# Second sample group's value tiles: four buffers of the key pool in place of the shared work pool

## The chip, the cores and the metric

One NeuronCore of one Trainium2 chip runs the whole program. The metric is device time in microseconds (us), from the start to the end of one execution; the figure that counts is the median of several executions. Beside it stands one execution that the hardware profiler recorded instruction by instruction; every row below is of that one.

## The reference

The program is one inference step of a decoder layer for a prompt (1 sequence of 512 tokens) and a sample group (8 sequences, b = 0..7, with 4 new tokens each), 1024 wide: a half-weighted SwiGLU block, then dilated attention (8 heads of 64) beside an S5 state-space group, a second half-weighted SwiGLU block, a gated projection and a final norm. The change concerns the attention of the sample group over its cache of 2048 old positions:

```
for window, dil in ((128, 1), (512, 4), (2048, 16)):
    idx = past + t - arange(window // dil + 1) * dil      # keys that new token t sees in this branch
    logits = q[t] . k_ext[idx] / 8 + bias ;  probs = softmax(logits)
    o = sum(probs * v_ext[idx])
merged = softmax-weighted sum of the three branches' o
```

So every sample sequence needs, of its cached values, the last 128 rows, and per new token 128 rows 4 apart and 128 rows 16 apart.

## The kernel before

All activations stay on chip. The program goes through a first feed-forward part, a mixing part (projections, prompt attention, sample attention, S5), and a second feed-forward part with the final output. In the mixing part the order of work on TensorE, VectorE, ScalarE and GpSimd is written out by hand: a string ORDER names, one after the other, steps of generators, and each engine works through its own list strictly in that order. `M` and `E` are weight matmul tiles and their evacuation, `aq`, `at`, `ap` are the three steps of a unit of prompt attention (scores with softmax, transposes, values), `SQ` multiplies cached keys by queries, `O0` and `O1` are the sample outputs of the sequences 0 to 3 and 4 to 7 (`sample_out(0)` and `sample_out(1)`, 15 steps each).

`sample_out(gr)` first makes the softmax weights of its four sequences (tiles `pz` and `sc`), then goes through nine value steps, n = 0 to 8: step 0 is the last 128 rows, steps 1 to 8 are (token, branch) pairs. Each step has two value tiles `vv` of 128 x 2 x 512 floats (512 KB), one for each pair of sequences, loaded by a DMA that GpSimd issues (line 1178). They are called 0a, 0b, 1a, 1b, ... 8a, 8b below. In step n the program first issues load n+1 (both tiles), and then TensorE multiplies the weights with both tiles of step n into one accumulator `po` (line 1191). Since a DMA is issued by GpSimd's own in-order list, a load whose buffer is not yet free holds up all that GpSimd has behind it; behind the loads of the second group stand only two `bt` loads (bias rows of prompt attention, line 1003, between 0b and 1a) and, much later, additions of the next norm.

Where a tile lies is decided by its pool. `wk` takes from a pool of six buffers (`wkp`, WK = 6) that also serves the S5 tiles earlier and `pz`; `kk2` takes from a pool of four buffers of the same size (`kkp`), used until then by the stream of cached keys in `SQ`, whose last multiplication stands before the second group's value steps. A new tile takes a buffer that its last tile has given back in program order, and its load waits until that tile's last reader is done. One of the six work buffers is held by the second group's `pz` until its last value step. The lines in question:

```python
        kkp = st.enter_context(tc.tile_pool(name="kkp", bufs=4))
        wk = lambda shape, name: wkp.tile(shape, F32, name=name, tag="wk")
        kk2 = lambda name: kkp.tile([P, 2, DA], F32, name=name, tag="kk")
```

Of the kernel before, what the change touches and what calls it, by code (L numbers as in the profile page):

```python
# [18 lines left out]
P = 128  # L19
# [9 lines left out]
DA = 512  # L29
# [73 lines left out]
def decoder_step(ctx: ExitStack, tc: tile.TileContext, a: dict, o: list):  # L103
# [3 lines left out]
    def dram(t, off, dims):  # L107
        return bass.AP(tensor=t.tensor, offset=t.offset + off, ap=dims)
# [6 lines left out]
    def sb(pool, shape, name, dt=F32, **kw):  # L115
        return pool.tile(shape, dt, name=name, **kw)
# [195 lines left out]
    def s2(shape, name, dt=F32):  # L312
        return cur["s2"].tile(shape, dt, name=name, tag="s2")

    def psm(shape=None, name="sm"):
        return cur["sm"].tile(shape or [P, 512], F32, name=name, tag="sm")
# [425 lines left out]
    with ExitStack() as st:  # L742
# [7 lines left out]
        wk = lambda shape, name: wkp.tile(shape, F32, name=name, tag="wk")  # L750
        s5 = lambda shape, name: sp5.tile(shape, F32, name=name, tag="s5")
        kk2 = lambda name: kkp.tile([P, 2, DA], F32, name=name, tag="kk")
# [380 lines left out]
        def sample_out(gr):  # L1133
            sc = scs[gr]
            s3 = lambda i, n=P: sc[:n, i].rearrange("p b (t h) -> p (b t) h", h=NH)
            bq = lambda t: t[:, None, :].to_broadcast([P, 16, NH])
            fs = lambda i, n=P: sc[:n, i].rearrange("p b x -> p (b x)")
            V.tensor_tensor(s3(0), s3(0), bq(bfar), ALU.add)
            V.tensor_tensor(s3(1), s3(1), bq(bnear), ALU.add)
            mx = s2([P, P], "mx")  # L1140
            V.tensor_tensor(mx, fs(1), fs(2), ALU.max)
            V.tensor_tensor(mx, mx, fs(0), ALU.max)
            V.tensor_tensor(mx[:NS], mx[:NS], fs(3, NS), ALU.max)
            yield
            ps = psm()
            PE.transpose(ps[:, :P], mx, ident)
            m1 = sb(small, [P, 4], "m1", bufs=2)
            V.tensor_reduce(m1[:, 0:1], ps[:, :P], AX.X, ALU.max)
            dg = sb(small, [P, P], "diag", bufs=2)
            V.tensor_scalar(dg, ident, m1[:, 0:1], None, ALU.mult)  # L1150
            yield
            pm = psm()
            PE.matmul(pm[:, :P], ones, dg, start=True, stop=True)
            for i, n_ in ((0, P), (1, P), (2, P), (3, NS)):
                V.tensor_tensor(fs(i, n_), fs(i, n_), pm[:n_, :P], ALU.subtract)
            pz = wk([P, 2, 4, 160], "pz")
            pz = [pz[:, i] for i in range(2)]
            dv = lambda t: t.rearrange("p b (t x) -> p b t x", x=40)[:, :, :, 0:8]
            s4v = lambda i, n=P: sc[:n, i].rearrange("p b (t h) -> p b t h", h=NH)
            for i in range(2):  # L1160
                V.memset(pz[i], 0.0)
                A.activation(dv(pz[i]), s4v(i), AF.Exp)
            A.activation(fs(2), fs(2), AF.Exp)
            A.activation(fs(3, NS), fs(3, NS), AF.Exp)
            yield
            su = s2([P, 4, 4, 8], "su")
            V.tensor_tensor(su, s4v(2), dv(pz[1]), ALU.add)
            V.tensor_tensor(su, su, dv(pz[0]), ALU.add)
            V.tensor_tensor(su[:NS], su[:NS], s4v(3, NS), ALU.add)
            order = [None] + [(j, f) for j in range(DS) for f in range(2)]  # L1170
            vld = {}

            def load(n):
                if n < len(order):
                    r0, step = (1920, 1) if n == 0 else ((order[n][0], 16), (1536 + order[n][0], 4))[order[n][1]]
                    vld[n] = [wk([P, 2, DA], "vv") for _ in range(2)]
                    for e in range(2):
                        Q.dma_start(vld[n][e], dram(cv, ((4 * gr + 2 * e) * PAST + r0) * DA,  # L1178
                                                    [[step * DA, P], [PAST * DA, 2], [1, DA]]))
            load(0)  # L1180
            yield
            ps = psm()
            PE.matmul(ps[:, 0:1], su.rearrange("p b t h -> p (b t h)"), ones[:, 0:1], start=True, stop=True)
            V.reciprocal(m1[:, 1:2], ps[:, 0:1])
            po = psm([P, 512], "po")
            for n, jf in enumerate(order):
                load(n + 1)
                v_ = vld.pop(n)
                for b in range(4):
                    lt = sc[:, 2, b] if n == 0 else pz[jf[1]][:, b, 32 * jf[0]:32 * jf[0] + 32]  # L1190
                    PE.matmul(po[32 * b:32 * b + 32, :], lt, v_[b // 2][:, b % 2, :], start=n == 0, stop=n == len(order) - 1)  # L1191
                if n == 0:
                    for b in range(4):
                        PE.matmul(po[32 * b:32 * b + 32, :], sc[:NS, 3, b], vs, start=False, stop=False)
                yield
            rv = s2([P, NH, HD], "rvv")
            V.scalar_tensor_tensor(rv, po.rearrange("p (h d) -> p h d", d=HD), m1[:, 1:2],
                                   sel_h[:, :, None].to_broadcast([P, NH, HD]), ALU.mult, ALU.mult)
            yield
            pf = psm([P, 4, 16], "pf")  # L1200
            for m in range(4):
                PE.matmul(pf[:, m, :], rv[:, 2 * m:2 * m + 2, :].rearrange("p h d -> p (h d)"), sel_t, start=True, stop=True)
            V.tensor_copy(att[:, :, S + 16 * gr:S + 16 * gr + 16], pf)
            yield
# [274 lines left out]
```

## Time and profile before

| | us |
|---|---|
| median of 3 runs | 1298.36 |
| lowest and highest | 1295.39, 1302.9 |
| the profiled execution's own time | 1290.02 |
| its span, first to last instruction | 1288.2 |
| TensorE busy in it | 1208.3 (94%) |
| mean granted TensorE clock | 0.968 |

The profiled execution is 8.3 us under the median and 5.4 us under the lowest of the three runs, so a sum of stalls read from it is compared with its own 1290.02 and then carried over to the median. Times in rows are us from the start of its span. The names PE, DVE, ACT, POOL and SP stand for TensorE, VectorE, ScalarE, GpSimd and SyncE; the second sample group's value steps lie between 719 and 764 us.

### The profile page before, as it was taken

To read this page: it belongs to the slowest core of one execution; us is meant where nothing else is said; L and a number is where in the kernel's file an instruction comes from. 1 tells how busy PE (TensorE), PEld (TensorE's weight loads), DVE (VectorE), ACT (ScalarE), POOL (GpSimd) and SP (SyncE) were. 2 spreads that over 40 slices of the span, in tenths; PEclk is the share of its full clock that TensorE was granted. 3 is DMA by queue.
4 is the path that set the end of the run, shared out by engine and by line. 5 is a ranking of instruction groups with operands and counts; after the bars stand their busy time and mean duration, and the time that the engine had idled before them with its cause. 6 is when DMAs were issued, how large, how long until landed. Compare 5 with 4: busy or idle time off the path is not lost.

```text
span 1288.2 us, 23223 instructions
## 1 busy us (share of the span) xinstructions
PE 1208.3 (94%) x9518; PEld 1142.4 (89%) x9518; DVE 713.5 (55%) x1499; ACT 446.1 (35%) x889; POOL 121.8 (9%) x195
## 2 busy tenths in 40 slices
PE   8999999999999999994769889999999999999995
PEld 7899999999999988983645449999999999999994
DVE  5544478476447638777775548444433444444455
ACT  5333322322233323121754445333322223333344
POOL 2200000233000112110123311000000000000000
PEclk8999999999999998996979989999999999999998
DMA  8484566668546549766358855445566455222321
GB/s 248 134 260 147 173 217 226 227 198 258 191 167 207 170 138 299 233 203 218 91 207 243 255 172 191 155 144 199 174 217 231 153 192 180 80 83 77 93 64 70
DMA packets 207547, 231.30 MB, mean 180 GB/s; under 512 B 8647, under 2 KB 187735, under 8 KB 206416
## 3 DMA queue, kind: packets, MB, share of 16 engines
q1 hardware_dynamic: 189552, 170.35, 40.8%
q0 software_dynamic: 17856, 59.45, 14.3%
q8 instruction: 75, 1.23, 0.4%
q14 instruction: 32, 0.26, 0.1%
q10 hardware_dynamic: 32, 0.01, 0.0%
HBM read 217.46 MB, written 81.89 MB: 232 GB/s over the span
## 4 chain that ended last, share of the span: by engine, by line
PE 81%; DMA 6%; DVE 5%; issue 4%; ACT 3%; POOL 1%; SPq 0%; ACTq 0%; POOLq 0%; DVEq 0%
PE acc L194 72%; DMA vv<-in_cache_v_dram 2%; DMA raw<-in_w_in_dram 1%; PE acc L206 1%; PE acc L1441 1%; DVE kk L1099 1%; DMA raw<-in_ffn_w_up_dram 1%; DMA pc<-pD 1%; PE sm L915 1%; PE po L1191 1%; DMA mm<-mD 1%; PE sm L910 1%; PE sm L263 1%; POOL vv L1178 1%; ACT L L1022 1%
## 5 line engine op out<-in xcount | busy, mean ns | idle before, releaser
L194 PE MATMUL acc<-xh,whi 128*128 128x272 f32 x1888 | 398.5, 292 | 5.9 <-DVE qT L773 1.3
L194 PE MATMUL acc<-xl,whi 128*128 128x272 f32 x1888 | 393.9, 290 | 0.7 <-DVE xl L304 0.3
L194 PE MATMUL acc<-xh,wlo 128*128 128x272 f32 x1888 | 393.4, 289 | 0.9 <-DVE wlo L176 0.9
L175 ACT CAST whi<-raw 128x512 fp32r<-128x512 f32 (+2 forms) x348 | 208.3, 606 | 531.1 <-PE acc L194 462.0
L176 DVE TENSOR_TENSOR wlo<-raw,whi 128x512 fp32r<-128x512 f32 (+2 forms) x348 | 231.1, 671 | 200.7 <-ACT whi L175 198.2
L194 PEld LDWEIGHTS acc<-xh,whi 128*128 128x128 f32 x1888 | 297.4, 189 | 12.0 <-issue 4.0
L194 PEld LDWEIGHTS acc<-xl,whi 128*128 128x128 f32 x1888 | 299.0, 190 | 1.9 <-DVE xl L304 0.8
L194 PEld LDWEIGHTS acc<-xh,wlo 128*128 128x128 f32 x1888 | 297.7, 189 | 1.4 <-DVE wlo L176 1.3
L194 PE MATMUL acc<-hh,whi 128*128 128x272 f32 x704 | 145.7, 288 | 0.0
L194 PE MATMUL acc<-hh,wlo 128*128 128x272 f32 x704 | 145.3, 288 | 0.0
L194 PE MATMUL acc<-hl,whi 128*128 128x272 f32 x704 | 145.2, 288 | 0.0
L194 PEld LDWEIGHTS acc<-hh,whi 128*128 128x128 f32 x704 | 110.7, 188 | 0.0
L194 PEld LDWEIGHTS acc<-hh,wlo 128*128 128x128 f32 x704 | 110.7, 188 | 0.0
L194 PEld LDWEIGHTS acc<-hl,whi 128*128 128x128 f32 x704 | 110.5, 188 | 0.0
L362 DVE TENSOR_TENSOR s<-acc,rstd 128x544 f32<-128x544 f32 x44 | 31.9, 724 | 87.3 <-PE acc L194 87.3
L356 DVE TENSOR_TENSOR s<-acc,rstd 128x544 f32<-128x544 f32 x44 | 31.9, 724 | 72.1 <-PE acc L194 65.9
L303 ACT CAST hh<-s 128x544 fp32r<-128x544 f32 x44 | 28.5, 647 | 78.9 <-DVE s L363 78.9
L304 DVE TENSOR_TENSOR hl<-s,hh 128x544 fp32r<-128x544 f32 x44 | 31.9, 725 | 27.3 <-ACT hh L303 27.3
L370 DVE SCALAR_TENSOR_TENSOR x<-acc,x 128x544 f32<-128x544 f32 x32 | 23.2, 725 | 36.0 <-PE acc L194 36.0
L1099 DVE TENSOR_TENSOR kk<-kk,qb 128x1024 f32<-128x1024 f32 x32 | 38.9, 1217 | 5.6 <-DMA qb<-qD 5.6
L1100 DVE TENSOR_REDUCE sc<-kk 128x16 f32<-128x1024 f32 x32 | 39.0, 1220 | 1.1
L357 ACT ACTIVATE s<-s 128x544 f32<-128x544 f32 x44 | 29.0, 659 | 11.5 <-DVE s L356 11.2
(397 smaller groups left out, 1116.6 us busy)
## 6 DMA issues: line engine op xcount, KB each, us to landing
out_dram<-in_cache_k_dram SPq DMA_DIRECT2D x32, 1022.0 KB, 7.0
out_dram<-in_cache_v_dram SPq DMA_DIRECT2D x32, 1022.0 KB, 6.0
raw<-in_ffn_w_gate_dram SPq DMA_DIRECT2D x44, 512.0 KB, 4.0
raw<-in_ffn_w_up_dram SPq DMA_DIRECT2D x44, 512.0 KB, 4.0
vv<-in_cache_v_dram POOLq DMA_DIRECT2D x36, 512.0 KB, 6.4
raw<-in_ffn_w_down_dram SPq DMA_DIRECT2D x32, 512.0 KB, 3.8
kk<-in_cache_k_dram POOLq DMA_DIRECT2D x32, 512.0 KB, 5.8
raw<-in_w_in_dram SPq DMA_DIRECT2D x16, 512.0 KB, 8.8
```

The costliest lines, as they stand in the source:

```text
L175: A.copy(hi[:, :len(p), :], r)
L176: V.tensor_tensor(lo[:, :len(p), :], r, hi[:, :len(p), :].bitcast(F32), ALU.subtract)
L194: PE.matmul(ps[:, h, :HT], wt[:, j, :], z[:, h * HT:(h + 1) * HT], start=done == 0 and n == 0, stop=done == len(ks) - 1 and n == 2)
L206: PE.matmul(ps[:, h, :HT], wt[:, j, :], z[:, h * HT:(h + 1) * HT], start=hf == 0 and j == 0 and n == 0, stop=hf == 1 and j == 3 and n == 2)
L303: A.copy(hi, src)
L304: V.tensor_tensor(lo, src, hi.bitcast(F32), ALU.subtract)
L356: V.tensor_tensor(v2(g1), pg[:, :, :HT], v2(rstd()), ALU.mult)
L357: A.activation(g1, g1, AF.Silu)
L362: V.tensor_tensor(v2(u1), pu[:, :, :HT], v2(rstd()), ALU.mult)
L370: V.scalar_tensor_tensor(v2(x[:, m, :]), ps[:, :, :HT], 0.5, v2(x[:, m, :]), ALU.mult, ALU.add)
L1099: V.tensor_tensor(t_, t_, qbs[n // 2], ALU.mult)
L1100: V.tensor_reduce(scs[b // 4][:, f, b % 4, 16 * jp:16 * jp + 16], t_.rearrange("p f (h d) -> p (f h) d", d=HD), AX.X, ALU.add)
```

## The change

The value tiles of the second group (`gr` = 1) are taken from the key stream's pool of four buffers; those of the first group stay in the work pool.

```diff
             def load(n):
                 if n < len(order):
                     r0, step = (1920, 1) if n == 0 else ((order[n][0], 16), (1536 + order[n][0], 4))[order[n][1]]
-                    vld[n] = [wk([P, 2, DA], "vv") for _ in range(2)]
+                    vld[n] = [kk2("vv") if gr else wk([P, 2, DA], "vv") for _ in range(2)]
                     for e in range(2):
                         Q.dma_start(vld[n][e], dram(cv, ((4 * gr + 2 * e) * PAST + r0) * DA,
                                                     [[step * DA, P], [PAST * DA, 2], [1, DA]]))
```

No instruction is added, removed or moved: every engine's list is the same as before. What differs is what the loads wait for. The rows below are POOL's, in program order, with the semaphores that each waits for: PE, DVE and Activation are other engines' progress, DMASW0 to DMASW7 are the landing marks that POOL's DMAs use in turn (0a has DMASW0, 0b DMASW1, the two `bt` 2 and 3, 1a 4, 1b 5, 2a 6, 2b 7, 3a again 0), DMAHW those of SP's DMAs. A load that names an older load's mark together with PE takes over that load's buffer once PE has read it.

At the start of the second group: vv_7865 and vv_7866 are 8a and 8b of the first group, vv_7939 and vv_7940 are 0a and 0b of the second.

```order
 L1178 DMA vv_7865<-in_cache_v_dram 128x2x512 [waits DMASW1_49,PE_49]
 L1178 DMA vv_7866<-in_cache_v_dram 128x2x512 [waits DMASW2_49,PE_49]
-L1178 DMA vv_7939<-in_cache_v_dram 128x2x512 [waits DMASW4_49,PE_49]
-L1178 DMA vv_7940<-in_cache_v_dram 128x2x512 [waits DMASW5_49,PE_49]
+L1178 DMA vv_7939<-in_cache_v_dram 128x2x512
+L1178 DMA vv_7940<-in_cache_v_dram 128x2x512 [waits DVE_49]
```

0a and 0b no longer wait for PE's reading of the first group's step 7; 0a waits for nothing, 0b for a key multiplication on DVE.

Behind the two `bt`, before: 1a, 1b (vv_8001, vv_8002), 2a, 2b (vv_8013, vv_8014), 3a, 3b (vv_8035, vv_8036), 4a, 4b (vv_8114, vv_8115).

```order
L1178 DMA vv_8001<-in_cache_v_dram 128x2x512 [waits DMASW6_49]
L1178 DMA vv_8002<-in_cache_v_dram 128x2x512 [waits DMASW7_49]
L1178 DMA vv_8013<-in_cache_v_dram 128x2x512 [waits DMAHW7_49,DMAHW4_49,DMAHW0_49]
L1178 DMA vv_8014<-in_cache_v_dram 128x2x512 [waits DMASW0_49,PE_49]
L1178 DMA vv_8035<-in_cache_v_dram 128x2x512 [waits DMASW1_49,PE_49]
L1178 DMA vv_8036<-in_cache_v_dram 128x2x512 [waits DMASW4_49,PE_49]
L1178 DMA vv_8114<-in_cache_v_dram 128x2x512 [waits DMASW5_49,DMASW2_49,PE_49]
L1178 DMA vv_8115<-in_cache_v_dram 128x2x512 [waits DMASW6_49,DMASW3_49,PE_49]
```

The same eight loads with the change:

```order
L1178 DMA vv_8001<-in_cache_v_dram 128x2x512 [waits DMASW4_49,DVE_49]
L1178 DMA vv_8002<-in_cache_v_dram 128x2x512 [waits DMASW5_49,DVE_49]
L1178 DMA vv_8013<-in_cache_v_dram 128x2x512 [waits DMASW6_49,DMASW0_49,PE_49]
L1178 DMA vv_8014<-in_cache_v_dram 128x2x512 [waits DMASW7_49,DMASW1_49,PE_49]
L1178 DMA vv_8035<-in_cache_v_dram 128x2x512 [waits DMASW4_49,PE_49]
L1178 DMA vv_8036<-in_cache_v_dram 128x2x512 [waits DMASW5_49,PE_49]
L1178 DMA vv_8114<-in_cache_v_dram 128x2x512 [waits DMASW6_49,DMASW2_49,PE_49]
L1178 DMA vv_8115<-in_cache_v_dram 128x2x512 [waits DMASW7_49,DMASW3_49,PE_49]
```

Before, a load takes over the buffer of the fifth load ahead of it (2b that of 0a, 3a that of 0b, 3b that of 1a, 4a that of 1b, and so on), and 2a names no value tile's mark; with the change each takes over the buffer of the fourth load ahead (2a that of 0a, 2b that of 0b, 3a that of 1a, up to 8b, that of 6b).

## Rows read from the trace of the kernel before

**Rows 1.** The page: span, and the chain that ended last, by line.

```profile
span 1288.2 us, 23223 instructions
...
PE acc L194 72%; DMA vv<-in_cache_v_dram 2%; DMA raw<-in_w_in_dram 1%; PE acc L206 1%; PE acc L1441 1%; DVE kk L1099 1%; DMA raw<-in_ffn_w_up_dram 1%; DMA pc<-pD 1%; PE sm L915 1%; PE po L1191 1%; DMA mm<-mD 1%; PE sm L910 1%; PE sm L263 1%; POOL vv L1178 1%; ACT L L1022 1%
```

**Rows 2.** Timeline of POOL, 716 to 758 us: start, us, instruction [idle before <-releaser].

```profile
716.96 0.72 POOL L1178 DMA_DIRECT2D vv<-in_cache_v_dram  x1 [3.59 <-PE po L1191]
719.91 1.42 POOL L1178 DMA_DIRECT2D vv<-in_cache_v_dram  x2 [2.24 <-PE sm L1146]
...
731.79 1.42 POOL L1178 DMA_DIRECT2D vv<-in_cache_v_dram  x2 [4.57 <-PE po L1191]
733.77 1.42 POOL L1178 DMA_DIRECT2D vv<-in_cache_v_dram  x2 [0.57 <-PE po L1191]
...
739.65 0.71 POOL L1178 DMA_DIRECT2D vv<-in_cache_v_dram  x1 [3.00 <-PE po L1191]
746.41 2.83 POOL L1178 DMA_DIRECT2D vv<-in_cache_v_dram  x4 [6.05 <-PE po L1191]
```

**Rows 3.** Timeline of PE, 721 to 764 us, columns as in rows 2.

```profile
721.91 1.05 PE L1191 MATMUL po<-vv,pz 128*32 128x512 f32 x4 [1.05 <-DMA vv<-in_cache_v_dram]
...
734.57 1.05 PE L1191 MATMUL po<-vv,pz 128*32 128x512 f32 x4
738.28 1.05 PE L1191 MATMUL po<-vv,pz 128*32 128x512 f32 x4 [2.66 <-DMA vv<-in_cache_v_dram]
...
745.05 1.92 PE L1191 MATMUL po<-vv,pz 128*32 128x512 f32 x16
...
751.71 1.93 PE L1191 MATMUL po<-vv,pz 128*32 128x512 f32 x8
...
755.49 1.48 PE L1191 MATMUL po<-vv,pz 128*32 128x512 f32 x8
...
758.88 1.09 PE L1048 MATMUL sm<-ident,L 128*128 128x128 f32 x8 [1.11 <-ACT qT L1063]
759.90 1.06 PE L1191 MATMUL po<-vv,pz 128*32 128x512 f32 x8
...
761.70 1.92 PE L1191 MATMUL po<-vv,pz 128*32 128x512 f32 x8
```

**Rows 4.** Tile vv, five stretches: issue durations and first, last start; issue to landing.

```profile
L1178 POOL DMA_DIRECT2D vv<-in_cache_v_dram x2: 704/716/727, 711.9 to 712.7; - x2
DMA to landing us min/median/max: 5.3/5.6/5.9
L1178 POOL DMA_DIRECT2D vv<-in_cache_v_dram x1: 707/707/707, 732.5 to 732.5; - x1
DMA to landing us min/median/max: 7.2/7.2/7.2
L1178 POOL DMA_DIRECT2D vv<-in_cache_v_dram x4: 704/712/718, 746.4 to 748.5; - x4
DMA to landing us min/median/max: 4.1/7.1/8.7
L1178 POOL DMA_DIRECT2D vv<-in_cache_v_dram x1: 704/704/704, 747.1 to 747.1; - x1
DMA to landing us min/median/max: 6.1/6.1/6.1
L1178 POOL DMA_DIRECT2D vv<-in_cache_v_dram x3: 707/718/718, 753.9 to 756.9; - x3
DMA to landing us min/median/max: 4.9/5.5/5.7
```

**Rows 5.** Three stretches: us, busy of PE, PEld, DVE, ACT, POOL; granted clock, DMA share, GB/s.

```profile
733.70:737.10 3.40, 1.93 (x12) 0.69 (x10) 0.66 (x2) 1.39 (x3) 2.14 (x3) 1.00 0.92 178
747.30:750.70 3.40, 1.36 (x10) 0.69 (x8) 1.11 (x6) 2.07 (x7) 1.94 (x3) 1.00 0.81 229
750.70:754.20 3.50, 3.50 (x14) 0.72 (x14) 1.66 (x7) 2.20 (x7) 0.26 (x1) 0.51 0.99 220
```

## The prediction

> **What bounds the kernel now.** I read the page first, for the whole: by its chain of work TensorE's weight matmuls set 72% of the end, the landing of value tiles 2% and POOL's issuing of them 1% [rows 1]. So the change can only touch a few per cent of the span, in the one place where those tiles are loaded and read. That place I read in two timelines beside each other, POOL's (when each load leaves) and PE's (when its tile is needed). POOL is a waiter here: it idles 4.57, 3.00 and 6.05 us until PE has read an older tile, and then sends one, two or four loads at once [rows 2]. PE in turn waits for landings: 2.66 us ahead of 2b at 738.28, and it loses some in steps 6 and 8, which take 1.48 and 1.92 us where an undisturbed step takes 1.06 [rows 3]. PE frees a buffer, POOL issues, the tile lands some 4 to 9 us later [rows 4], PE reads it. That loop sets the pace of the stage, together with the softmax chain of prompt attention on ACT, which holds PE for 1.11 us before 758.88 [rows 3]. How early a load may leave depends on the number of buffers, so I follow the loop load by load.
>
> **The change part by part.** Durations are of the profiled execution, whose time is 1290.02 us (span 1288.2 and 1.8 around it).
>
> *The first pair leaves earlier.* 0a and 0b now have no PE to wait for, so they leave right behind the first group's 8b, at 716.96 + 0.72 = 717.7 instead of 719.91 [rows 2]. Nothing is gained by it: PE goes from 721.91 to the end of 2a's matmuls at 735.62 without a wait for a value tile [rows 3], so 0a and 0b had already landed in time. A small loss is possible, since 8b had its queue to itself: it was issued at 716.96 and read at 721.91, after 4.9 us, and PE stood waiting for it 1.05 us, whereas the first of a pair sent together needed 5.3 [rows 4]. Bounds 0 and 0.4; I take **0.4**, the row of the pair.
>
> *One buffer fewer in the loop.* Each load from 2a on now needs the buffer of the fourth load ahead, not the fifth. Four loads of the list shift into places whose times are known:
> - 2a now waits for step 0, as 2b did; 2a and 2b leave at 731.79 and 732.50, where 2b and 3a left before [rows 2]. The load that left at 732.50 took 7.2 us [rows 4], so 2b would land at 739.7 and be read there instead of at 738.28 [rows 3]: **+1.4**. Bounds: as second of a pair in an empty queue it takes 5.9, which gives +0.1; with the longest 8.7 it is +2.9. I take 7.2 because it is the same place in the same queue at the same time.
> - 3a and 3b wait for step 1 and leave at 733.77 and 734.5; even with the longest landing, 8.7, both are there at 743.2, and step 3 starts at 745.05 + 1.4. Nothing. 4a leaves at 739.65 (after 2a's half, as 5a did after 2b), 4b 1.4 later at 741.1, landing after 6.1 at 747.2; PE is at step 4 at about 747.4. **0**, or +0.9 if it needs 7.2.
> - 5a, 5b, 6a, 6b wait for steps 3 and 4 and leave as a burst of four, as 5b, 6a, 6b, 7a did at 746.41 [rows 2], 1.4 later. The burst's second landed after 6.1 and its fourth after 8.7 [rows 4]. So 5b lands at 747.12 + 6.1 + 1.4 = 754.6, where PE is at step 5 at 753.1. Its second half (1.05) ends at 755.7, against 753.64 before: the shift is now 2.0, **+0.6** (0 with 5.3, +1.2 with half-speed matmuls). 6b lands at 748.53 + 8.7 + 1.4 = 758.6 and step 6 ends at 759.7, 0.7 behind its shifted time; the 1.11 us for which PE then waits for ACT [rows 3] hide that. Without the cover it would be +0.7.
> - 7a and 7b wait for step 5 and leave at 756.0 and 756.7; 7b lands after 5.5 [rows 4] at 762.2 while PE comes to step 7 at 761.9: **+0.3** (0 to 0.8). 8b waits for the end of step 6, 759.7, leaves at 760.0, lands after 5.7 at 765.7, and step 8 ends at 766.7 against 763.62 before: a total shift of 3.1, so **+0.8**.
>
> The sum is 0.4 + 1.4 + 0.6 + 0.3 + 0.8 = **+3.5 us**. Nothing takes it back, because all that follows step 8 on PE (the last attention values and the output weights) stands behind it in order. Behind the waiting loads POOL has nothing but additions of the next norm, and the two `bt` loads stand ahead of 1a and keep their own wait, so nothing else is held up. The low bound of the sum is +0.5 (pairs land in 5.3 and 5.9, only 8b's later release remains), the high one about +6 with the upper ends of all terms.
>
> One rule speaks against a stall of this size. The landings in this stage took 4.1 to 8.7 us [rows 4]. The Trainium skill (page "DMA: Bandwidth & Descriptors", section "Anatomy of one DMA — SWDGE (gpsimd) path") gives about 2.0 us plus the bytes over 436 GB/s, which would be an estimate of 3.2 us for 512 KB; 2b would then land at 735.7, no term of the sum would remain, and the change would cost nothing. The trace disagrees, since not one landing in these rows is that short.
>
> **The rivals.**
> 1. *Hidden anyway.* With fewer loads in flight each may land faster: a pair in a quiet queue took 5.3 and 5.9 [rows 4], and between 733.7 and 737.1 the DMA engines were 0.92 busy at only 178 GB/s [rows 5], which may not repeat. Then 2b comes at 732.5 + 5.9 = 738.4, and the total is +0 to +1.5, so 1298 to 1300. Against it: the four loads from 731.79 to 734.5 leave exactly when four left before; the first of those, issued at 731.79, was read at 738.28, 6.5 us later [rows 2, 3], and the second took 7.2.
> 2. *Slower, by the clock.* PE now runs dry at 734.57 instead of 735.62, since 2a is no longer there, and until 738.2: 3.7 us in place of 2.66. The 2.66 us left the granted clock at 1.00, its 2.4 GHz level, while the stretch from 747.3 to 750.7, in which PE was busy 1.36 of 3.40 us and so idle 2.04, was followed by one at 0.51, nearly all at 1.2 GHz, up to 754.2 [rows 5]. There step 5 took 1.93 us against 1.06 [rows 3]. A stretch of 3.5 us at that level loses about 1.7 us of work. One more such stretch makes +5.2, two make +6.9, that is 1305, and from there on it is slower by over 0.5%. Against it: such a stretch now falls in the sparse part anyway, and the one of before may move rather than be joined. The Trainium skill (page "TensorE: Matmul & The Clock Gate", section "HAM oscillation — how this bites in real kernels") says that matmuls which wait for DMAs lose their full clock again and again; by it the slow end is the right one. The trace agrees only in part: the idling that a slow stretch followed here was not ahead of a value tile, and the wait for one did not bring it.
> 3. *Faster.* The work pool's loads no longer compete with the first group's, and 0a and 0b leave 2.2 us earlier. It would need PE to have waited for step 0 or 1, and step 2's first half at 734.57 has no idle time before it either [rows 3]; the most to win is the 1.05 us of waiting at 721.91, which is not for a tile of this group.
>
> **How the numbers follow.** Stall without further loss of clock: chance 0.45, +3.5. Hidden: 0.22, 0 to +1.5. Clock: 0.28, +5 to +7. Faster: 0.05 with all that I have not seen. What a measurement of this kernel can tell from no change is about 0.5%, 6.5 us. Carried from the profiled 1290.02 to the median 1298.36, the likeliest is 1301.9. The range takes in the hidden case and the clock case with the spread of the runs (-3.0 and +4.5 about the median): 1295.4 to about 1309. Slower by over 0.5% is most of the clock case's upper half plus a little of the stall's high bound, 0.2; faster by that much 0.03; the rest, 0.77, is within 0.5%.
>
> **What would show it.** Right: in POOL's timeline of the changed kernel 0a and 0b leave at about 717.7, 2a and 2b (not 2b and 3a) at about 731.8, and four at once near 748; PE's wait ahead of step 2's tiles begins at 734.6 and ends near 739.7 in two pieces; step 8 ends near 767. Wrong: if 2b lands before 738.4 the first term falls and most of the sum with it; if PE's idle time before the output weights is unchanged, the attention chain on ACT covers more than I gave it; if the stretches at 0.5 between 734 and 775 last much over 10 us in all, the clock decides and the time is above 1304.

## The result: 1305.69 us, and the profile after

| | before | with the change |
|---|---|---|
| median, us | 1298.36 | 1305.69 |
| lowest to highest of 7 runs, us | 1295.26 to 1303.58 | 1299.97 to 1316.27 |
| ratio, 95% interval | | 1.0069 (1.004 to 1.0099) |

So the change costs about 9 us (5 to 13 by the interval; 7.3 between the medians), 2.1 to 2.6 times the 3.5 us of the likeliest case and inside the range. The runs lean to the side to which I had given 0.2: slower by over 0.5%, though the interval begins a little under that.

The page of the changed kernel, its span and its chain by line:

```profile
span 1307.7 us, 23229 instructions
...
PE acc L194 72%; DMA vv<-in_cache_v_dram 3%; DMA raw<-in_w_in_dram 2%; PE acc L206 1%; PE po L1191 1%; PE acc L1441 1%; DMA raw<-in_ffn_w_up_dram 1%; DMA pc<-pD 1%; DVE kk L1099 1%; PE sm L263 1%; PE sm L915 0%; PE sm L1014 0%; POOL vv L1178 0%; DVE sc L1100 0%; PE sm L910 0%
```

The line that should answer to the change is the landing of value tiles, 3% of the chain where it was 2% [rows 1]; a step of one per cent says little by itself, since the landing of `raw<-in_w_in_dram`, which the change does not touch, went from 1% to 2% as well. The span itself is 19.5 us longer, but 12.4 us of that lie ahead of PE's wait for the first group's 8b (735.50 - 2.23 against 721.91 - 1.05), where both kernels do the same; only the stage can be compared. Its loads, in the timeline of POOL (start, us, instruction, idle before and what ended it):

```profile
729.38 2.12 POOL L1178 DMA_DIRECT2D vv<-in_cache_v_dram  x3 [4.08 <-PE po L1191]
738.82 1.17 POOL L1003 DMA_DIRECT2D bt<-btD  x2 [7.31 <-ACT pt L1050]
739.98 1.43 POOL L1178 DMA_DIRECT2D vv<-in_cache_v_dram  x2
746.64 1.41 POOL L1178 DMA_DIRECT2D vv<-in_cache_v_dram  x2 [5.24 <-PE po L1191]
748.63 1.41 POOL L1178 DMA_DIRECT2D vv<-in_cache_v_dram  x2 [0.58 <-PE po L1191]
754.96 0.70 POOL L1178 DMA_DIRECT2D vv<-in_cache_v_dram  x1 [4.91 <-PE po L1191]
758.27 0.72 POOL L1178 DMA_DIRECT2D vv<-in_cache_v_dram  x1 [2.61 <-PE po L1191]
765.69 2.82 POOL L1178 DMA_DIRECT2D vv<-in_cache_v_dram  x4 [6.70 <-PE po L1191]
```

This is the pattern that was forecast: 8b of the first group, 0a and 0b in one go of three; then only 1a and 1b behind the `bt`, where three loads had left; 2a and 2b together, 3a and 3b, 4a and 4b apart, and 5a to 6b as a burst. What PE got from it (timeline of PE):

```profile
735.50 1.92 PE L1191 MATMUL po<-vv,pz 128*32 128x512 f32 x4 [2.23 <-DMA vv<-in_cache_v_dram]
737.35 1.54 PE L1048 MATMUL sm<-ident,L 128*128 128x128 f32 x6
...
752.72 1.92 PE L1191 MATMUL po<-vv,pz 128*32 128x512 f32 x4 [3.23 <-DMA vv<-in_cache_v_dram]
756.04 1.92 PE L1191 MATMUL po<-vv,pz 128*32 128x512 f32 x4 [1.40 <-DMA vv<-in_cache_v_dram]
757.89 0.80 PE L1014 MATMUL sm<-kT,qT 64*128 64x128 f32 x4
758.62 1.42 PE L1061 MATMUL po<-pt,vt 128*64 128x128 f32 x16
...
764.32 1.92 PE L1191 MATMUL po<-vv,pz 128*32 128x512 f32 x16
...
774.77 1.94 PE L1191 MATMUL po<-vv,pz 128*32 128x512 f32 x8
...
783.35 1.05 PE L1191 MATMUL po<-vv,pz 128*32 128x512 f32 x4 [0.95 <-DMA vv<-in_cache_v_dram]
```

Against [rows 3]: PE waits 2.23 us for the first group's 8b (before 1.05), and 3.23 + 1.40 for the two halves of step 2 (before 2.66 for the second half alone). From 8b's matmuls to the end of step 8 it takes 784.40 - 735.50 = 48.9 us, before 763.62 - 721.91 = 41.7; with the longer wait ahead of 8b the stage has grown by 8.4 us. That is about the measured cost, but it is the difference of two single executions, and the experiments show that the one of before makes it look larger than it is.

Tile vv, for the load at 729.38 (8b of the first group) and for the four from 746.64 on (2a to 3b): durations and starts of the issues, and landing times.

```profile
L1178 POOL DMA_DIRECT2D vv<-in_cache_v_dram x1: 716/716/716, 729.4 to 729.4; - x1
DMA to landing us min/median/max: 6.1/6.1/6.1
...
L1178 POOL DMA_DIRECT2D vv<-in_cache_v_dram x4: 704/710/716, 746.6 to 749.3; - x4
DMA to landing us min/median/max: 6.0/8.9/9.8
```

8b took 6.1 us where it had taken 4.9, and 2b (issued at 747.34, read at 756.04) 8.7 where I had put 7.2. Four stretches of the windows view (columns as in rows 5):

```profile
735.40:738.80 3.40, 3.30 (x12) 1.64 (x12) 0.75 (x1) 0.48 (x1) 0.00 (x0) 0.51 0.47 187
749.10:752.50 3.40, 0.39 (x4) 0.15 (x2) 0.11 (x2) 1.02 (x2) 0.94 (x2) 1.00 0.92 177
752.50:759.30 6.80, 5.18 (x18) 1.56 (x20) 0.55 (x4) 0.24 (x1) 1.42 (x2) 0.50 0.87 272
769.60:773.00 3.40, 3.40 (x14) 0.71 (x12) 1.21 (x5) 1.55 (x4) 0.00 (x0) 0.50 0.90 281
```

After both waits the granted clock is at its 1.2 GHz level, for 3.4 and 6.8 us; before, the clock stayed at 1.00 there and only fell at 750.7 [rows 5], to which the stretch from 769.60 corresponds here. That is why the halves of step 2 take 1.92 us and not 1.05.

### The profile page after: what moved, and what is told of

It is laid out like the page before. It is cut to its first block, busy times and chain, and to the rows that moved or that the text cites. A ratio compares the mean times of both kernels' runs of the same rounds, so it can differ in the third digit from the quotient of the medians.

```text
span 1307.7 us, 23229 instructions
## 1 busy us (share of the span) xinstructions
PE 1216.7 (93%) x9518; PEld 1146.1 (88%) x9518; DVE 713.6 (55%) x1499; ACT 446.1 (34%) x889; POOL 121.4 (9%) x195
## 4 chain that ended last, share of the span: by engine, by line
PE 80%; DMA 8%; DVE 4%; issue 4%; ACT 2%; POOL 1%; SPq 0%; ACTq 0%; POOLq 0%; DVEq 0%
PE acc L194 72%; DMA vv<-in_cache_v_dram 3%; DMA raw<-in_w_in_dram 2%; PE acc L206 1%; PE po L1191 1%; PE acc L1441 1%; DMA raw<-in_ffn_w_up_dram 1%; DMA pc<-pD 1%; DVE kk L1099 1%; PE sm L263 1%; PE sm L915 0%; PE sm L1014 0%; POOL vv L1178 0%; DVE sc L1100 0%; PE sm L910 0%
## 5 line engine op out<-in xcount | busy, mean ns | idle before, releaser
L1191 PE MATMUL po<-vv,pz 128*32 128x512 f32 x128 | 26.8, 673 | 11.3 <-DMA vv<-in_cache_v_dram 11.2
```

## The experiments

Theory: the pace of the stage is set by how many buffers the loads can run ahead with; losing one costs the time. Rivals: the early first pair, the place in the key pool, the rows that are read, the clock. Ratios are to the kernel before on the same chip, with 95% intervals.

| run | ratio | interval |
|---|---|---|
| five buffers, early pair | 1.0014 | 0.9992 to 1.0037 |
| four buffers in the work pool | 1.0065 | 1.0041 to 1.0088 |
| alternate pools (nine) | 0.9991 | 0.9963 to 1.0019 |
| the change, contiguous rows | 0.9983 | 0.996 to 1.0006 |
| before, contiguous rows | 0.9993 | 0.9968 to 1.0019 |
| the change, rows 4 apart made contiguous | 1.0008 | 0.9982 to 1.0034 |
| the change, rows 16 apart made contiguous | 1.0056 | 1.0031 to 1.0081 |
| first pair in the work pool, rest in the key pool | 0.9973 | 0.9947 to 1.0 |
| thirds | 0.9997 | 0.9974 to 1.002 |
| the change, wait filled with matmuls | 1.0056 | 1.0027 to 1.0084 |
| only the first pair in the key pool | 0.9998 | 0.9971 to 1.0025 |

**Five buffers again.**

```diff
-vld[n] = [kk2("vv") if gr else wk([P, 2, DA], "vv") for _ in range(2)]
+vld[n] = [kk2("vv") if gr and (2 * n + e) % 5 < 4 else wk([P, 2, DA], "vv") for e in range(2)]
```

> The key pool's four buffers and, for every fifth value tile, one of the work pool: each load again waits for the fifth load ahead of it, as before, while 0a and 0b still leave early. Theory (the number of buffers sets the pace): 2b leaves where it left before, and the time is that of the kernel before within 3 us, ratio 0.998 to 1.003; what the early 0a and 0b cost behind the first group's 8b would be seen alone, at most 1 to 2 us. Rival (the place in the key pool or the early pair costs the time): as slow as the changed kernel, ratio 1.005 to 1.009.

Measured 1.0014. With the fifth buffer the cost is gone to within 0.4%, although four of the five lie in the key pool and 0a and 0b leave early: neither the place nor the early pair makes up the cost. PE at the first group's 8b and at 2b:

```profile
727.63 1.92 PE L1191 MATMUL po<-vv,pz 128*32 128x512 f32 x4 [2.22 <-DMA vv<-in_cache_v_dram]
745.04 1.92 PE L1191 MATMUL po<-vv,pz 128*32 128x512 f32 x4 [2.53 <-DMA vv<-in_cache_v_dram]
```

Both waits are followed by half-speed work here too. From the wait for 8b to the end of step 8 this profile has 47.7 us, 5.0 more than that of the kernel before (42.8) and 3.4 less than that of the changed one (51.1). The time is nevertheless that of before, so the profile of before shows its stage at its best rather than as it usually runs: of 98 further executions of that kernel only one took less than the profiled 1290.02 us.

**One buffer of the work pool held.**

```diff
+            if gr:
+                hold = wk([P, 2, DA], "hold")
+                V.memset(hold[:, 0, 0:1], 0.0)
             load(0)
...
+            if gr:
+                V.tensor_copy(m1[:, 2:3], hold[:, 0, 0:1])
             rv = s2([P, NH, HD], "rvv")
```

> All value tiles in the work pool as before, but one of its buffers is held by an unused tile through the second group's value steps, so four are left for them; it adds two operations of one column on VectorE, about 0.2 us in all, and 0a and 0b still wait for the first group's last steps. Theory (number of buffers): the same pairs as in the changed kernel (2a with 2b, four loads at once later), 2b lands 6.5 to 8.7 us after its issue, ratio 1.003 to 1.008. Rival (early pair or place): no slower than before, ratio 0.998 to 1.002.

Measured 1.0065. Four buffers in the old place, with the first pair as late as before, cost what the change costs. PE's timeline there (line 1194 is line 1191 of the other kernels), at 8b of the first group and at step 2:

```profile
724.61 1.05 PE L1194 MATMUL po<-vv,pz 128*32 128x512 f32 x4 [1.29 <-DMA vv<-in_cache_v_dram]
...
740.30 1.92 PE L1194 MATMUL po<-vv,pz 128*32 128x512 f32 x4 [2.90 <-DMA vv<-in_cache_v_dram]
743.74 1.92 PE L1194 MATMUL po<-vv,pz 128*32 128x512 f32 x4 [1.52 <-DMA vv<-in_cache_v_dram]
```

The two waits of step 2 and the slow clock in it are those of the changed kernel; the wait for 8b is nearly that of before.

**Alternate pools.**

```diff
+vld[n] = [kk2("vv") if gr and n % 2 == 0 else wk([P, 2, DA], "vv") for _ in range(2)]
```

> Even steps take the key pool, odd steps the work pool: nine buffers, so no load waits for a step less than four steps ahead, and the loads leave in bursts as soon as POOL comes to them. Theory: the three waits for value tiles of the second group in the kernel before (2.66, 0.4 and 0.9 us) vanish, 2 to 5 us less than before, ratio 0.996 to 0.999. Rival (the softmax chain on ScalarE or the rate of the transfers sets the pace of the stage): same as before, ratio 0.999 to 1.002, with waits for ScalarE grown by as much.

Measured 0.9991, no difference that can be told; the theory's gain did not come. Here no load waits for step 0, and 2a to 3b leave together at 734.95 to 737.05, yet PE still waits at step 2, and half-speed work follows:

```profile
743.20 1.05 PE L1191 MATMUL po<-vv,pz 128*32 128x512 f32 x4
746.83 1.92 PE L1191 MATMUL po<-vv,pz 128*32 128x512 f32 x4 [2.57 <-DMA vv<-in_cache_v_dram]
```

2b is late with nine buffers as with five. So a buffer theory alone is not enough: something else makes this load slow. The stage is 48.3 us here by its profile, 5.5 more than before, and again the time does not show it.

**Contiguous rows**, in the changed kernel and in the one before.

```diff
-r0, step = (1920, 1) if n == 0 else ((order[n][0], 16), (1536 + order[n][0], 4))[order[n][1]]
+r0, step = (1920, 1) if n == 0 or gr else ((order[n][0], 16), (1536 + order[n][0], 4))[order[n][1]]
```

> The changed kernel, but every value step of the second group reads the last 128 rows in place of rows 4 or 16 apart, so the sample output of sequences 4 to 7 is not the reference's; sizes, waits and order are unchanged. Theory (a burst lands slowly because several loads share the queue): 2b lands 7 to 9 us after its issue as in the changed kernel, ratio to the kernel before 1.004 to 1.009. Rival (rows 4 or 16 apart are read slowly): 2b lands in 6.2 us or less, the wait ahead of it shrinks by 1.5 us or more, ratio 0.998 to 1.003.

> The kernel before with every value step of the second group reading the last 128 rows (its sample output for sequences 4 to 7 is not the reference's). It is the partner of the changed kernel with the same rows, which ran at ratio 0.9983. If the fifth buffer matters only because rows read apart land slowly, both are alike: ratio 0.996 to 1.000. If the number of buffers costs time at any speed of landing, this one is faster than its partner by 4 us or more: ratio under 0.995.

Measured 0.9983 and 0.9993. The changed kernel loses all its cost when the rows are contiguous, and the kernel before gains nothing from it: four buffers and five are then alike. Landing of 2a to 3b in the changed kernel with contiguous rows, and PE at step 2:

```profile
DMA to landing us min/median/max: 4.0/4.8/5.6
```

```profile
744.00 1.05 PE L1191 MATMUL po<-vv,pz 128*32 128x512 f32 x4 [1.22 <-DMA vv<-in_cache_v_dram]
745.35 1.05 PE L1191 MATMUL po<-vv,pz 128*32 128x512 f32 x4 [0.29 <-DMA vv<-in_cache_v_dram]
```

The same four loads, issued at the same distances, land in 4.0 to 5.6 us and not in 6.0 to 9.8, and 2b is read 1.35 us behind 2a and not 3.32. One thing besides the distance of the rows differs: every step now reads the 128 rows that step 0 has read before. No run tells the two apart.

**Which rows.** The changed kernel with only the steps 4 apart, then only those 16 apart, made contiguous (`n == 0 or gr and order[n][1] == 1`, then `== 0`).

> The changed kernel; only the steps that read rows 4 apart (2, 4, 6, 8) read the last 128 rows instead, so the output is not the reference's. If rows 4 apart are the slow ones: step 2's second tile lands 1.4 us behind its first instead of 3.3, ratio 0.997 to 1.002. If rows 16 apart are: nothing changes at step 2, ratio 1.004 to 1.009.

> The changed kernel; only the steps that read rows 16 apart (1, 3, 5, 7) read the last 128 rows instead, so the output is not the reference's. If rows 4 apart are the slow ones: 2b still lands 8 us or more after its issue, ratio 1.004 to 1.009. If rows 16 apart are: ratio 0.997 to 1.002.

Measured 1.0008 and 1.0056. PE at step 2 in the first, then in the second kernel:

```profile
745.59 1.05 PE L1191 MATMUL po<-vv,pz 128*32 128x512 f32 x4 [1.44 <-DMA vv<-in_cache_v_dram]
746.93 1.05 PE L1191 MATMUL po<-vv,pz 128*32 128x512 f32 x4 [0.29 <-DMA vv<-in_cache_v_dram]
```

```profile
744.85 1.85 PE L1191 MATMUL po<-vv,pz 128*32 128x512 f32 x4 [2.77 <-DMA vv<-in_cache_v_dram]
748.23 1.92 PE L1191 MATMUL po<-vv,pz 128*32 128x512 f32 x4 [1.53 <-DMA vv<-in_cache_v_dram]
```

It is the steps that read rows 4 apart: 2, 4, 6 and 8. With them contiguous 2b follows 2a by 1.34 us; with them as they are it follows by 3.38, whatever the other steps read. The distance of the rows alone does not do it, though. 6a and 6b of the changed kernel, rows 4 apart too and sent 0.7 us apart, landed after 7.2 and 7.8 us, so 1.3 us behind each other:

```profile
DMA to landing us min/median/max: 7.2/7.5/7.8
```

**Only the first pair in the work pool.**

```diff
+vld[n] = [kk2("vv") if gr and n else wk([P, 2, DA], "vv") for _ in range(2)]
```

> 0a and 0b in the work pool, all later tiles in the key pool: 2a and 2b find free buffers and leave right behind 1a and 1b, and from step 3 on each load waits for the fourth ahead of it, as in the changed kernel; 0a and 0b wait as before. If the loss sits at step 2, its waits of 3.2 and 1.4 us are gone and the ratio is 0.997 to 1.002; if it comes from the later steps as much, 1.003 to 1.008.

Measured 0.9973. Four buffers from step 1 on, but 2a and 2b find theirs free and leave right behind 1b, where POOL idled 5.24 us in the changed kernel. PE at the first group's 8b, at step 2 and at step 8:

```profile
728.82 1.05 PE L1191 MATMUL po<-vv,pz 128*32 128x512 f32 x4 [1.07 <-DMA vv<-in_cache_v_dram]
...
741.49 1.75 PE L1191 MATMUL po<-vv,pz 128*32 128x512 f32 x8
...
748.95 3.00 PE L1191 MATMUL po<-vv,pz 128*32 128x512 f32 x16
...
768.36 1.05 PE L1191 MATMUL po<-vv,pz 128*32 128x512 f32 x4 [1.07 <-DMA vv<-in_cache_v_dram]
```

Step 2 has 0.7 us of waiting left (1.75 for the 1.06 of an undisturbed step), and no slow clock behind it; from its start to that of step 3 it is 7.5 us, before 10.5 (745.05 - 734.57). Steps 3 to 8, which have the four buffers of the change, do lose something: steps 3 and 4 take 3.00 us for 1.92, and to the end of step 8 it is 20.5 us, as in the changed kernel (20.1) and not as before (18.6). The time shows the sum of both. The kernel with one buffer held also has the late pair and four buffers from step 3 on; apart from the pools it differs at step 2 alone, and runs at 1.0065 against 0.9973. So the loss that can be measured sits at step 2.

**Thirds.**

```diff
+vld[n] = [kk2("vv") if gr and n % 3 else wk([P, 2, DA], "vv") for _ in range(2)]
```

> Steps 0, 3 and 6 take the work pool, the others the key pool: 0a and 0b leave as late as before, and after them no load has to wait for a step less than two steps back. Theory: no wait ahead of step 2, no slow clock behind it, and the first group's 8b lands after about 4.9 us again; ratio 0.995 to 0.999, like the run with only the first pair in the work pool (0.9973) or a little under it. Rival (that gain was chance): 0.999 to 1.002.

Measured 0.9997: the gain of the last run was not repeated by a kernel that has more buffers. With all of 1a to 3b in the queue at once 2b comes late again, with a wait of 2.14 us. The loads from 1a to 2b leave at the same times as in the last run (732.0 to 734.1), in the same order; with 3a and 3b right behind them 2b lands after 10.5 us in place of 8.0.

```profile
744.67 1.15 PE L1191 MATMUL po<-vv,pz 128*32 128x512 f32 x4 [2.14 <-DMA vv<-in_cache_v_dram]
```

No version here is shown to beat the kernel before; the interval of the best one ends at 1.0.

**The wait filled with matmuls.**

```diff
                 v_ = vld.pop(n)
+                if gr and n == 2:
+                    pfl = psm()
+                    for _ in range(10):
+                        PE.matmul(pfl[:, :P], ones, ones, start=True, stop=True)
```

> The changed kernel with ten more matmuls of 128x128 on TensorE, whose result nobody reads, in front of step 2's value matmuls, about 2 to 2.5 us of work in a wait of 3.2 us. If the slow clock after that wait costs 1 to 2 us by itself: step 2's second half and the attention matmuls behind it run at full clock (1.05 us in place of 1.92 for the half), ratio 1.003 to 1.006. If the clock is not what costs, or the fill gets in the way: 1.006 to 1.010.

Measured 1.0056, and inconclusive for the clock: the fill shortened the idle time ahead of 2a to 0.88 us, but 2b came 2.21 us after, and the half-speed stretch merely began there:

```profile
748.24 1.92 PE L1195 MATMUL po<-vv,pz 128*32 128x512 f32 x4 [2.21 <-DMA vv<-in_cache_v_dram]
```

**Only the first pair in the key pool.**

```diff
+vld[n] = [kk2("vv") if gr and not n else wk([P, 2, DA], "vv") for _ in range(2)]
```

> Only 0a and 0b in the key pool, all later tiles in the work pool: the pair leaves early, right behind the first group's 8b, and nothing else waits longer than before (2a and 2b do not wait at all). Theory (the early pair slows 8b): 8b lands after 6 us in place of 4.9, and the stretch up to step 1 is 1 to 2.4 us longer than in the kernel before, partly made up by the missing wait at step 2; ratio 0.999 to 1.002, above that of the run with the first pair in the work pool (0.9973). Rival (8b's slower landing is chance): 8b lands in 5.2 us or less, ratio 0.995 to 0.998.

Measured 0.9998. By time alone it can't be told from the run with the pair the other way round (0.9973; the intervals overlap). In the trace the pair's cost is there: PE waits 2.45 us for the first group's 8b, which took 6.6 us.

```profile
732.22 1.05 PE L1191 MATMUL po<-vv,pz 128*32 128x512 f32 x4 [2.45 <-DMA vv<-in_cache_v_dram]
```

Over all profiles, 8b of the first group landed after 4.9 to 5.7 us in the five kernels where 0a and 0b leave late, and after 6.0 to 7.4 us in the eight where they leave right behind it.

## Why the prediction was right in its mechanism and too small in its size

The stage's 8.4 us, from the two timelines: 1.2 more waiting for 8b, 1.5 of half-speed work behind that wait (the half of 8b 1.92 for 1.05, the transposes behind it 1.54 for 0.87), of which 0.2 is made up on the way to step 2, 2.0 more waiting at step 2 (3.23 + 1.40 - 2.66), 2.4 up to step 3, which is again half-speed work, and 1.5 from step 3 to the end of step 8 (784.40 - 764.32 = 20.1 against 763.62 - 745.05 = 18.6). The stages of five buffers and of alternate pools are 5.0 and 5.5 us longer than that of before by the same reading, and their times are not measurably longer; so this split says where the changed kernel's profile loses, not what each part costs in the medians.

- *0a and 0b leave early and gain nothing.* Right. The price on 8b was the term "0.4, the row of the pair"; it measured 1.2, and the clock fell behind it. I took the first load of a pair as the model, and here three loads left in one go. In the times this price does not show: early pair and five buffers ran at 1.0014 and 0.9998, late pair and four buffers at 1.0065.
- *One buffer fewer shifts the loads by one place.* Right in the order, as POOL's timeline shows, and shown by time: four buffers in the work pool cost 1.0065, five in mixed pools 1.0014.
- *"2b lands after 7.2, because it is the same place in the same queue at the same time": +1.4.* This is the term that was too small. The place in the queue alone does not decide; which rows are read and what leaves beside it do. With the change the two tiles of step 2, with rows 4 apart, leave together, and the second is slow. 2b took 8.7 and its tile followed 2a's by 3.3 us, against 1.35 with contiguous rows. The waits of step 2 grew by 2.0 us in place of 1.4.
- *Steps 3 to 8: 0 + 0.6 + 0.3 + 0.8 = 1.7.* The profile has 1.5, but from other parts, so the near match is luck. Steps 5 and 7 lose nothing (forecast 0.6 and 0.3); step 6 loses 0.5 by 6b (1.94 against 1.48), of which the wait for ACT behind it takes back 0.1, where I had it hide all; step 8 loses 1.1 (forecast 0.8). What these steps cost in the medians was not shown by a run of its own.
- *The clock as a rival of 0.28.* It came, in the profiled execution, in addition to the likeliest case: two stretches of 3.4 and 6.8 us at its half-speed level where before there was none, about 3.7 us of the 8.4 by the split above. My sign for it was stretches that last much over 10 us between 734 and 775, and a time above 1304: they last 13.6 us (3.4, 6.8 and 3.4), in the kernel before 10.3, and the median is 1305.69. A stretch at 1.2 GHz follows step 2's wait in the changed kernel and in the runs with five, with held, with alternate and with thirds buffers, with 16-apart rows made contiguous and with the fill, which waited 2.1 us or more there; in none of those that waited 1.5 us or less, and not in the kernel before, with its 2.66. The length of the wait alone does not decide it: behind 8b the stretch came after 2.1 to 2.2 us in four kernels and after 3.06 in a fifth, and not after 2.45 (only the first pair in the key pool) or 3.08 (the fill). That the clock by itself costs these microseconds was not shown by a run: the one made for it only moved the stretch, and the kernels with five buffers and with alternate pools have both stretches and are not measurably slower than before.
- *Hidden anyway (0.22).* Not so with the rows as they are, and not because fewer loads were in flight; with contiguous rows 2a to 3b land in 4.0 to 5.6 us and the cost of the lost buffer vanishes. The Trainium skill (page "DMA: Bandwidth & Descriptors", section "Anatomy of one DMA — SWDGE (gpsimd) path") had given an estimate of 3.2 us. The traces do not agree: the shortest landings in this stage are about 4 us, with contiguous rows (4.0) and with rows 16 apart (4.1, [rows 4]).
- *Faster.* No sign of it.
- *Nothing takes it back.* Right: from the end of step 8 to the matmuls ahead of the output weights it is 4.8 us in both kernels (768.45 - 763.62 and 789.22 - 784.40). The sign that I gave for the contrary, an unchanged idle time before the output weights, was the wrong way about: that idle time is 2.47 us before and 2.46 with the change, and the whole delay of step 8 is passed on.

## What to carry to other kernels

The number of buffers costs nothing by itself; it costs where a slow load can no longer leave early enough. So price a lost buffer with the landing time of that very tile, with its rows and with the loads that will leave beside it, not with that of whatever load stood in that place of the queue; here even tiles with equal row distance landed 1.3 or 3.4 us behind each other. Look also whether a load issued sooner than needed slows the one in front that is waited for. And before a stage is split by two profiles, see where each lies among the executions: kernels whose profiled stage was 5 us longer ran in the same time.

## What the runs showed of the hardware

- 512 KB tiles of 2 KB rows, 128 from each of two sequences: at step 2, sent together, the second landed 3.3 to 3.4 us behind the first with rows 4 apart (8 KB) in four kernels (the change, one held, 16 apart made contiguous, the fill), and about 1.35 us behind it with contiguous rows. Other pairs with rows 4 apart that left together landed 1.3 us apart (step 6 of the changed kernel, step 4 with five buffers), or 2.0 (step 2 with the first pair in the work pool). Why step 2 is slow stays open: whether it is the distance, rows read for the first time, or the loads beside it was not separated.
- A load that has two others sent right behind it landed about 1 us later (8b: 6.0 to 7.4 us in place of 4.9 to 5.7 over 13 profiles), and 2b 2.5 us later (10.5 in place of 8.0).
- A wait of 2.5 to 2.7 us at 2b was followed by a stretch at 1.2 GHz in two kernels and not in a third.
- Running further ahead did not help: with nine buffers the loads of steps 2 and 3, all sent at once, landed after 8.1 to 13.7 us,

```profile
DMA to landing us min/median/max: 8.1/12.1/13.7
```

and step 2 waited as long as with five.
